# The first norm by token chunks, and the splits of the last merge written two groups later

## The chip, the cores and the metric

One core of a Trainium2 chip runs the kernel. Its engines work side by side: TensorE (PE, matmuls; PEld its weight loads), VectorE (DVE), ScalarE (ACT) and GpSimd (POOL); SyncE (SP) issues most loads. The metric is the device time of one execution in microseconds, the median of several runs. 2331.54 us was measured before the change.

## The reference

One inference step through two layers over 1088 tokens (1024 of a prompt, 64 of eight samples with eight tokens each) and 1024 channels. A layer is:

```python
shift, scale, gate = split(silu(c) @ w_ada + b_ada, 3)
h = rmsnorm(x, norm_g) * (1 + scale) + shift          # rmsnorm: x * rsqrt(mean(x*x) + eps) * g
qa, ka, va, ga, ub, vb, gb, qc, fc, ic, gc, ma, mb, mc = split_cols(h @ w_in)
ya, yb, yc = window_attention(...), spatial_gating(...), hgrn2(...)
merged = sigmoid(ma) * ((ya * silu(ga)) @ w_br_a) + sigmoid(mb) * ((yb * silu(gb)) @ w_br_b) \
       + sigmoid(mc) * ((yc * silu(gc)) @ w_br_c)
x = x + gate * (merged @ w_out)
```

c is one vector for the prompt and one for each sample, so shift, scale and gate have 9 columns: one for all prompt tokens, eight for the samples' tokens. All is float32.

## The kernel before

Activations lie with channels on the 128 partitions and tokens along the free dimension. The 1024 channels are 8 tiles (k = 0 to 7); the 1088 tokens are three chunks (`CH`): chunk 0 and 1 have 384 tokens, chunk 2 has 256 prompt tokens and the 64 sample tokens. A float32 product is made of three fast matmuls (`mm3`, L379 to L381): weights and activations are each split into a high and a low part. For weights a `piece` is cast on ACT (L342) and its low part subtracted on DVE or POOL (L343); for activations `split` does the same (L456 on ACT, L457 on DVE). `H[c]` holds both parts of the normed input of chunk c.

**Order of the work.** POOL and SP follow the program's order throughout (`ORDERED`). PE, DVE and ACT are ordered by a planner with a time model of its own: an engine that is free there gets a ready instruction, and the place in the program ranks those that are ready together. Inside `with tc.manual_schedule(...)` the instructions of PE, DVE and ACT also keep the written order among themselves; those written outside the block may come between them. On the chip each engine then runs its list strictly in order and waits where an operand isn't there. Buffers are rotated: 17 slabs of 1152 columns, 4 raw weight tiles (`wr`), 4 small tiles (`gq`), 4 + 4 banks of PSUM.

**The startup (layer 0).** SP loads the eight tiles of x whole (L1093). ACT squares each (L1096, L1099) and DVE adds the squares up (L1100). `rstd` sums over the partitions with matmuls against a column of ones, one per 128 tokens and nine in all (L473), and finds 1/sqrt in a dozen small DVE steps (L477 to L238). `spread_rows` brings one chunk's factors back over all partitions: a product with the identity on DVE (L489) and a matmul with ones (L491); ACT copies that to `rbs[c]` (L1137). The adaLN factors of channel tile k come from two weight tiles (`ada_load`, two loads of 512 KB), 32 matmuls (L290), an ACT copy (L272), two transposes (L277) and five small DVE operations (L280 to L286). The first unit's weights (`w_first`, four `wr` loads of 256 KB) are loaded ahead of the adaLN weights; POOL makes their low parts.

The loop over k then makes, for each chunk, `modulate` (DVE: x times scale times rbs, L500; for the 64 sample columns three POOL operations, L503 to L506) and `split_h` (ACT adds the shift into the high part, L513; DVE the low part, L514), asks for the adaLN factors of k + 2, and runs 18 matmuls for two output tiles and three chunks. The six sums stay in PSUM over all k. Afterwards the second unit follows with matmuls of another form (L433 to L435).

**The merge.** Three branches, in the order 2, 0, 1; for each 8 output tiles j and 3 chunks, 24 groups of 12 matmuls. After each group `ev_m` asks for a gate two groups ahead (POOL issues the load, L1518), multiplies the gate with the sum in PSUM (DVE, L1549) and adds it to `merged` (POOL, L1550; DVE in the last j). In the third branch the finished tile is split at once (L456, L457), as the output projection's input. Four banks of PSUM hold the sums.

Of the kernel before, what the change touches and what calls it, by code (L numbers as in the profile page):

```python
# [14 lines left out]
AF = mybir.ActivationFunctionType  # L15
# [5 lines left out]
SEQ = 1024  # L21
NB = 8
TS = 8
NTOK = SEQ + NB * TS
# [3 lines left out]
CH = [(0, 384), (384, 384), (768, 320)]  # L28
# [120 lines left out]
def build(tc, i, o, L):  # L149
    nc = tc.nc  # L150
# [8 lines left out]
    V, S, G, T = nc.vector, nc.scalar, nc.gpsimd, nc.tensor  # L159
# [7 lines left out]
    def slab(n="s", dt=F32):  # L167
        return sp.tile([128, 1152], dt, tag="slab", name=uid(n))

    def small(n, w, dt=F32, bufs=2):  # L170
        return sm.tile([128, w], dt, tag=n, name=uid(n), bufs=bufs)
# [7 lines left out]
    def v3(ap, b):  # L179
        return ap.rearrange("p (a b) -> p a b", b=b)  # L180

    def bc_in(ap, n):
        s = list(ap.shape)
        return ap.unsqueeze(len(s)).to_broadcast(s + [n])
# [169 lines left out]
    def prep(parts, eng=V, keep=None):  # L354
        return [piece(p, eng, keep) for p in parts]
# [3 lines left out]
    units = []  # L359
# [24 lines left out]
    nxt = [0]  # L384
# [70 lines left out]
    def split(dst_h, dst_l, src):  # L455
        S.copy(dst_h, src)  # L456
        V.tensor_sub(dst_l, src, dst_h.bitcast(F32))  # L457
# [8 lines left out]
    def rstd(ssq, n):  # L466

        nf, r = n // 128, n % 128
        nt = nf + (r > 0)
        ps = bank("ss")  # L470
        for t in range(nt):
            w = min(128, n - t * 128)
            T.matmul(ps[0:w, t:t + 1], ssq[:, t * 128:t * 128 + w], ones[:, 0:1], start=True, stop=True)  # L473
        vv = small("nv", 9)
        if r:
            V.memset(vv[:, nf:nt], 1.0)
        V.tensor_scalar(vv[:, 0:nf], ps[:, 0:nf], 1.0 / D, EPS, ALU.mult, ALU.add)  # L477
        if r:
            V.tensor_scalar(vv[0:r, nf:nt], ps[0:r, nf:nt], 1.0 / D, EPS, ALU.mult, ALU.add)
        rs = small("nr", 9)  # L480
        rsqrt(vv[:, 0:nt], rs[:, 0:nt], nt)
        return rs

    def spread_rows(rs, n):

        nf, r = n // 128, n % 128
        nt = nf + (r > 0)
        dg = small("gq", 384, bufs=4)
        V.tensor_mul(v3(dg[:, 0:nt * 128], 128), bc_mid(ident, nt), bc_in(rs, 128))  # L489
        pb = bank("rb")  # L490
        T.matmul(pb[:, 0:nf * 128], ones, dg[:, 0:nf * 128], start=True, stop=True)  # L491
        if r:
            T.matmul(pb[:, nf * 128:n], ones[0:64, :], dg[0:64, nf * 128:n], start=True, stop=True)
        return pb

    def modulate(l, k, u, x, rb, t0, n):

        npr = max(0, min(n, SEQ - t0))
        adaT = ada_t[l]
        V.scalar_tensor_tensor(u[:, 0:npr], x[:, 0:npr], adaT[:, 8 + k, 0:1], rb[:, 0:npr], ALU.mult, ALU.mult)  # L500
        if npr < n:
            e = V if l else G
            e.tensor_mul(u[:, npr:n], x[:, npr:n], rb[:, npr:n])  # L503
            us = v3(u[:, npr:n], TS)
            e.tensor_mul(us, us, bc_in(adaT[:, 8 + k, 1:9], TS))
            e.tensor_add(us, us, bc_in(adaT[:, k, 1:9], TS))  # L506

    def split_h(l, k, Hc, u, t0, n):

        npr = max(0, min(n, SEQ - t0))  # L510
        sh = ada_t[l][:, k, 0:1]
        hi, lo = Hc[:, 0, k, :], Hc[:, 1, k, :]
        S.activation(hi[:, 0:npr], u[:, 0:npr], AF.Identity, bias=sh)  # L513
        V.scalar_tensor_tensor(lo[:, 0:npr], u[:, 0:npr], sh, hi[:, 0:npr].bitcast(F32), ALU.add, ALU.subtract)  # L514
        if npr < n:
            S.copy(hi[:, npr:n], u[:, npr:n])
            (V if l else G).tensor_sub(lo[:, npr:n], u[:, npr:n], hi[:, npr:n].bitcast(F32))
# [569 lines left out]


    ada_t = [cp.tile([128, 24, 9], F32, tag=f"adaT{l}", name=f"adaT{l}") for l in range(L)]
    X, ssq = [], slab("ssq")  # L1090
    for k in range(8):
        x = slab("x")
        nc.sync.dma_start(x[:, 0:NTOK], i["xT"][k])  # L1093
        X.append(x)
        if k == 0:
            S.activation(ssq[:, 0:NTOK], x[:, 0:NTOK], AF.Square)  # L1096
        else:
            sq = slab("sq")
            S.activation(sq[:, 0:NTOK], x[:, 0:NTOK], AF.Square)  # L1099
            V.tensor_add(ssq[:, 0:NTOK], ssq[:, 0:NTOK], sq[:, 0:NTOK])  # L1100
    ident = cst("ident", [128, 128])
    ada_consts(0)
    H = new_H()
    rbs = []

    def ada_load(k):
        ws = []
        for a in range(2):
            ws.append(v3(slab("wada")[:, 0:1024], 128))
            nc.sync.dma_start(ws[-1], i["w_ada"][0, 8 * a + k])  # L1110
        return ws

    def ada_both(ps, ws):
        for a in range(2):
            for e in range(2):
                ada_products(ps, a, e, ws[a][:, 4 * e:4 * e + 4])
# [5 lines left out]
            pass  # L1122

    with tc.manual_schedule(engines={ET.PE, ET.DVE, ET.Activation}):
        w_first = prep(units[0], G)
        nxt[0] = 1
        ada_w = [ada_load(0), ada_load(1)]
        rs = rstd(ssq, NTOK)
        ada_ps = bank("ada")
        ada_both(ada_ps, ada_w.pop(0))  # L1130
        for c, (t0, n) in enumerate(CH):
            pb = spread_rows(rs[:, 3 * c:3 * c + 3], n)
            rbs.append(small("gq", 384, bufs=4))
            if c == 0:
                for _ in ada_rows(0, [0, 8], ada_ps):
                    pass
            S.copy(rbs[c][:, 0:n], pb[:, 0:n])  # L1137
    ada_first(1, ada_w.pop(0))
    x_dram = i["xT"]

    for l in range(L):
# [11 lines left out]
        if l == 0:  # L1153

            pss = [[mbank() if m * 3 + c < 4 else bank("first") for c in range(3)] for m in range(2)]
            for k in range(8):
                for c, (t0, n) in enumerate(CH):
                    x = X[k][:, t0:t0 + n]
                    modulate(0, k, x, x, rbs[c], t0, n)
                    split_h(0, k, H[c], x, t0, n)  # L1160
                if k + 2 < 8:
                    ada_first(k + 2, ada_load(k + 2))
                for m in range(2):
                    for c, (t0, n) in enumerate(CH):
                        ps = pss[m][c]
                        rh, rl = rhs_h(c, k)
                        mm3(ps[:, 0:n], col(w_first, 8, m, k), (rh, rl), k == 0, k == 7)
                if k == 3:
                    prefetch()
            for m in range(2):  # L1170
                ev = ev_ga(yd[3][m])
                for c, (t0, n) in enumerate(CH):
                    ev(c, t0, n, pss[m][c][:, 0:n])
            del X, ssq, rbs, x, sq
            late_consts()
            lower_bounds()
            ada_consts(1)
# [14 lines left out]
        k, v = slab("ts"), slab("ts")  # L1192
# [314 lines left out]
        rhs_y = lambda k, c: [cols(t, c) for t in y0[k]]  # L1507


        merged, sgs = [], []  # L1510
        grp = [(b, j, c) for b in BR_ORDER for j in range(8) for c in range(3)]

        def load_gate():
# [7 lines left out]
        for b in range(3):  # L1521
            if b == 0:
                Hy = new_H()
                rhs_n = lambda k, c, Hy=Hy: (Hy[c][:, 0, k, :], Hy[c][:, 1, k, :])
                ly = gated_y(BR_ORDER[1], rhs_n)
                side.append(ly)
            elif b == 1:
                del y0
                y2 = []
                rhs_n = lambda k, c: [cols(t, c) for t in y2[k]]  # L1530
                ly = gated_y(BR_ORDER[2], y2)
                side.append(ly)
            else:
                del Hy
                Hm = new_H()
            for j in range(8):
                if j % 2 == 0:
                    w = unit()
                    M.first = True
                if b == 0:  # L1540
                    merged.append(slab("mg"))

                def ev_m(c, t0, n, ps):
                    load_gate()
                    sg, mg = sgs.pop(0), merged[j][:, t0:t0 + n]
                    if b == 0:
                        V.tensor_mul(mg, sg, ps)  # L1547
                        return
                    V.tensor_mul(sg, sg, ps)  # L1549
                    (V if b == 2 and j == 7 else G).tensor_add(mg, mg, sg)  # L1550
                    if b == 2:
                        split(Hm[c][:, 0, j, :], Hm[c][:, 1, j, :], mg)
                f_mtile(w, j % 2, 4, lambda c, k: rhs_y(k, c), ev_m)
            if b < 2:
                drain(ly)
                rhs_y = rhs_n
        del rhs_y, rhs_n, merged, ly, y2
        drain(*side)
        last = l + 1 == L
        if not last:  # L1560
# [88 lines left out]
```

## Time and profile before

| | us |
|---|---|
| median of 3 runs | 2331.54 (2329.98 to 2332.61) |
| profiled execution | 2331.8 |
| its span, first to last instruction | 2330.0 |
| PE busy | 2257.2 |
| DVE busy | 1273.0 |
| ACT busy | 799.4 |
| POOL busy | 611.5 |

The profile is one execution. The span leaves out 1.8 us around it. Busy time of PE is counted from issue to a modelled end and overlaps, so a count of matmuls in a stretch says more than its busy time. In a timeline row the first number is the start, the second the length, and the bracket says how long the engine had been idle and which instruction ended that.

### The profile page before, as it was taken

The numbers are of one execution on the slowest core, as the hardware profiler recorded it, in microseconds if no ns is written. First come the engines' busy times: TensorE is split into PE (matmuls) and PEld (weight loads), VectorE is DVE, ScalarE is ACT, GpSimd is POOL, SyncE is SP. The second block draws the span as 40 slices with busy tenths as digits, with TensorE's granted clock in tenths as the row PEclk, the third lists the DMA queues.
The fourth block names the chain that finished last, engine by engine and source line by source line (L and its number), as shares of the span: only waits on it lengthen the run. The fifth ranks groups of instructions, "written<-read, shape, count | busy, mean of one in ns | idle before, by whom it ended". The sixth has DMA issues, their size and how long they took to land.

```text
span 2330.0 us, 43307 instructions
## 1 busy us (share of the span) xinstructions
PE 2257.2 (97%) x17170; PEld 2142.1 (92%) x17170; DVE 1273.0 (55%) x2893; ACT 799.4 (34%) x2032; POOL 611.5 (26%) x691
## 2 busy tenths in 40 slices
PE   6999999999999999998999999999999999999998
PEld 5999899989999899997999988999899999999898
DVE  6557748575363435464573586576654633346431
ACT  4436622333133334122243465223331433332110
POOL 3101014242232322275110010132322332315621
PEclk9999999999999999999999999999999999999999
DMA  7222110203134445664422121112121323366541
GB/s 285 78 81 68 62 50 25 85 29 117 47 117 153 159 161 200 223 204 132 131 91 78 62 76 65 37 48 67 59 86 60 107 89 110 107 229 204 156 132 46
DMA packets 128442, 251.26 MB, mean 108 GB/s; under 512 B 19760, under 2 KB 59952, under 8 KB 128208
## 3 DMA queue, kind: packets, MB, share of 16 engines
q1 hardware_dynamic: 87824, 156.46, 21.0%
q0 software_dynamic: 19680, 65.29, 8.4%
q10 hardware_dynamic: 20736, 26.75, 3.2%
q8 instruction: 135, 2.21, 0.4%
q14 instruction: 67, 0.55, 0.1%
HBM read 185.13 MB, written 65.27 MB: 107 GB/s over the span
## 4 chain that ended last, share of the span: by engine, by line
PE 65%; DVE 11%; issue 9%; POOL 8%; DMA 3%; ACT 2%; SPq 1%; POOLq 0%; DVEq 0%; ACTq 0%
PE mm L379 13%; PE mm L380 13%; PE mm L381 12%; PE mm L433 4%; POOL mg L1550 4%; PE mm L435 4%; PE mm L434 4%; PE c L379 2%; PE c L381 2%; PE c L380 2%; POOL gq L1518 1%; PE av L914 1%; DVE pc L343 1%; DMA wr<-in_w_in 1%; PE sc L877 1%
## 5 line engine op out<-in xcount | busy, mean ns | idle before, releaser
L379 PE MATMUL mm<-H,pc 128*128 128x384 f32 (+1 forms) x1872 | 626.5, 335 | 5.8 <-DVE gq L1549 4.7
L380 PE MATMUL mm<-H,pc 128*128 128x384 f32 (+1 forms) x1872 | 614.6, 328 | 0.0
L381 PE MATMUL mm<-H,pc 128*128 128x384 f32 (+1 forms) x1872 | 614.5, 328 | 0.0
L343 DVE TENSOR_TENSOR pc<-wr,pc 128x512 fp32r<-128x512 f32 x308 | 223.5, 739 | 295.8 <-ACT pc L342 294.7
L379 PEld LDWEIGHTS mm<-H,pc 128*128 128x128 f32 x1872 | 352.3, 188 | 27.2 <-issue 16.5
L380 PEld LDWEIGHTS mm<-H,pc 128*128 128x128 f32 x1872 | 352.6, 188 | 3.8 <-issue 3.2
L381 PEld LDWEIGHTS mm<-H,pc 128*128 128x128 f32 x1872 | 352.1, 188 | 1.1 <-DVE H L457 0.6
L433 PE MATMUL mm<-pc,H 128*128 128x256 f32 x896 | 259.0, 289 | 0.2 <-DVE gq L1150 0.2
L435 PE MATMUL mm<-pc,H 128*128 128x256 f32 x896 | 254.4, 284 | 0.0
L434 PE MATMUL mm<-pc,H 128*128 128x256 f32 x896 | 253.6, 283 | 0.0
L342 ACT CAST pc<-wr 128x512 fp32r<-128x512 f32 x312 | 189.7, 620 | 162.2 <-PE mm L381 80.0
L435 PEld LDWEIGHTS mm<-pc,H 128*128 128x128 f32 x896 | 171.6, 192 | 3.2 <-issue 3.2
L433 PEld LDWEIGHTS mm<-pc,H 128*128 128x128 f32 x896 | 171.6, 192 | 2.3 <-DVE gq L1150 0.5
L434 PEld LDWEIGHTS mm<-pc,H 128*128 128x128 f32 x896 | 171.7, 192 | 0.0
L379 PE MATMUL mm<-y,pc 128*128 128x384 f32 (+1 forms) x384 | 128.3, 334 | 15.7 <-DVE gq L1549 15.7
L381 PE MATMUL mm<-y,pc 128*128 128x384 f32 (+1 forms) x384 | 125.5, 327 | 0.0
L380 PE MATMUL mm<-y,pc 128*128 128x384 f32 (+1 forms) x384 | 125.3, 326 | 0.0
L1550 POOL TENSOR_TENSOR mg<-mg,gq 128x384 f32<-128x384 f32 (+1 forms) x90 | 103.4, 1149 | 77.1 <-DVE gq L1549 74.9
L457 DVE TENSOR_TENSOR tw<-wr,tw 128x512 fp32r<-128x512 f32 x80 | 65.6, 850 | 94.4 <-ACT tw L456 94.3
L631 POOL TENSOR_TENSOR hk<-hk,ht 128x512 f32<-128x512 f32 (+1 forms) x48 | 70.1, 1462 | 136.2 <-issue 39.8
L1151 POOL DMA_DIRECT2D y<-gq x48 | 26.4, 551 | 289.1 <-DVE gq L1150 116.3
L1518 POOL DMA_DIRECT2D gq<-g x144 | 79.2, 551 | 85.0 <-DVE mg L1547 50.4
(413 smaller groups left out, 4491.3 us busy)
## 6 DMA issues: line engine op xcount, KB each, us to landing
wr<-in_w_in SPq DMA_DIRECT2D x192, 256.0 KB, 3.3
yr<-y SPq DMA_DIRECT2D x40, 544.0 KB, 4.6
g<-gq ACTq DMA_DIRECT2D x96, 192.0 KB, 1.9
gq<-g POOLq DMA_DIRECT2D x96, 192.0 KB, 2.9
wada<-in_w_ada SPq DMA_DIRECT2D x64, 256.0 KB, 3.6
wr<-in_w_in SPq DMA_DIRECT2D x112, 128.0 KB, 2.5
wr<-in_w_br SPq DMA_DIRECT2D x48, 256.0 KB, 5.3
wada<-in_w_ada SPq DMA_DIRECT2D x16, 512.0 KB, 7.4
```

The source lines that it names most:

```text
L342: S.copy(pc[:, 0, :], flat)
L343: eng.tensor_sub(pc[:, 1, :], flat, pc[:, 0, :].bitcast(F32))
L379: T.matmul(ps, w[0], r[0], start=start, stop=False, skip_group_check=True)
L380: T.matmul(ps, w[1], r[0], start=False, stop=False, skip_group_check=True)
L381: T.matmul(ps, w[0], r[1], start=False, stop=stop, skip_group_check=True)
L433: T.matmul(p3(ps), a, wh[k], start=k == 0, stop=False)
L434: T.matmul(p3(ps), a, wl[k], start=False, stop=False)
L435: T.matmul(p3(ps), b, wh[k], start=False, stop=k == 7)
L457: V.tensor_sub(dst_l, src, dst_h.bitcast(F32))
L631: G.tensor_mul(kv[:, :, 0, :], kv[:, :, 0, :], bc_in(tv[:, :, 1], m))
L1518: nc.gpsimd.dma_start(sgs[-1], gd[b][j][:, t0:t0 + n])
L1550: (V if b == 2 and j == 7 else G).tensor_add(mg, mg, sg)
```

## The change

1. x is loaded chunk by chunk (`x_load`), 24 loads instead of 8. Chunk 0 comes first, then the adaLN weights of k = 0, chunk 1, the adaLN weights of k = 1, the first unit's weights, chunk 2.
2. Squares, sums, `rstd` and the spreading run once per chunk (`x_stats`), in written order: chunk 0, then the adaLN factors of k = 0 and the casts of the first weights, then chunk 1, then chunk 2.
3. Chunks 1 and 2 of all eight x tiles are multiplied with `rbs` by POOL, in place, 16 operations. In the loop ACT applies scale and shift in one Identity, in place, and the plain `split` follows. The sample columns keep two POOL operations per k. Chunk 0 is made as before.
4. In the third branch of the merge the split of a group is written after the evacuation of the group two later; the last two follow after the loop.

```diff
--- before.py
+++ after.py
@@ -1087,17 +1087,26 @@
 
 
     ada_t = [cp.tile([128, 24, 9], F32, tag=f"adaT{l}", name=f"adaT{l}") for l in range(L)]
-    X, ssq = [], slab("ssq")
-    for k in range(8):
-        x = slab("x")
-        nc.sync.dma_start(x[:, 0:NTOK], i["xT"][k])
-        X.append(x)
-        if k == 0:
-            S.activation(ssq[:, 0:NTOK], x[:, 0:NTOK], AF.Square)
-        else:
-            sq = slab("sq")
-            S.activation(sq[:, 0:NTOK], x[:, 0:NTOK], AF.Square)
-            V.tensor_add(ssq[:, 0:NTOK], ssq[:, 0:NTOK], sq[:, 0:NTOK])
+    X = [slab("x") for _ in range(8)]
+
+    def x_load(c):
+        t0, n = CH[c]
+        for k in range(8):
+            nc.sync.dma_start(X[k][:, t0:t0 + n], i["xT"][k][:, t0:t0 + n])
+
+    def x_stats(c):
+
+        t0, n = CH[c]
+        q = slab("ssq")[:, 0:n]
+        for k in range(8):
+            if k % 3 == 0:
+                sq = slab("sq")
+            d = sq[:, k % 3 * 384:k % 3 * 384 + n] if k else q
+            S.activation(d, X[k][:, t0:t0 + n], AF.Square)
+            if k:
+                V.tensor_add(q, q, d)
+        return rstd(q, n)
+    x_load(0)
     ident = cst("ident", [128, 128])
     ada_consts(0)
     H = new_H()
@@ -1122,19 +1131,27 @@
             pass
 
     with tc.manual_schedule(engines={ET.PE, ET.DVE, ET.Activation}):
-        w_first = prep(units[0], G)
-        nxt[0] = 1
-        ada_w = [ada_load(0), ada_load(1)]
-        rs = rstd(ssq, NTOK)
+        ada_w = [ada_load(0)]
+        x_load(1)
+        ada_w.append(ada_load(1))
         ada_ps = bank("ada")
-        ada_both(ada_ps, ada_w.pop(0))
         for c, (t0, n) in enumerate(CH):
-            pb = spread_rows(rs[:, 3 * c:3 * c + 3], n)
+            rs = x_stats(c)
+            if c == 0:
+                ada_both(ada_ps, ada_w.pop(0))
+            pb = spread_rows(rs[:, 0:3], n)
             rbs.append(small("gq", 384, bufs=4))
+            S.copy(rbs[c][:, 0:n], pb[:, 0:n])
             if c == 0:
                 for _ in ada_rows(0, [0, 8], ada_ps):
                     pass
-            S.copy(rbs[c][:, 0:n], pb[:, 0:n])
+                w_first = prep(units[0], G)
+                nxt[0] = 1
+                x_load(2)
+            else:
+                for k in range(8):
+                    x = X[k][:, t0:t0 + n]
+                    G.tensor_mul(x, x, rbs[c][:, 0:n])
     ada_first(1, ada_w.pop(0))
     x_dram = i["xT"]
 
@@ -1156,8 +1173,17 @@
             for k in range(8):
                 for c, (t0, n) in enumerate(CH):
                     x = X[k][:, t0:t0 + n]
-                    modulate(0, k, x, x, rbs[c], t0, n)
-                    split_h(0, k, H[c], x, t0, n)
+                    if c == 0:
+                        modulate(0, k, x, x, rbs[c], t0, n)
+                        split_h(0, k, H[c], x, t0, n)
+                        continue
+                    npr, at = min(n, SEQ - t0), ada_t[0]
+                    S.activation(x[:, 0:npr], x[:, 0:npr], AF.Identity, bias=at[:, k, 0:1], scale=at[:, 8 + k, 0:1])
+                    if npr < n:
+                        us = v3(x[:, npr:n], TS)
+                        G.tensor_mul(us, us, bc_in(at[:, 8 + k, 1:9], TS))
+                        G.tensor_add(us, us, bc_in(at[:, k, 1:9], TS))
+                    split(H[c][:, 0, k, :], H[c][:, 1, k, :], x)
                 if k + 2 < 8:
                     ada_first(k + 2, ada_load(k + 2))
                 for m in range(2):
@@ -1171,7 +1197,7 @@
                 ev = ev_ga(yd[3][m])
                 for c, (t0, n) in enumerate(CH):
                     ev(c, t0, n, pss[m][c][:, 0:n])
-            del X, ssq, rbs, x, sq
+            del X, rbs, x
             late_consts()
             lower_bounds()
             ada_consts(1)
@@ -1507,7 +1533,7 @@
         rhs_y = lambda k, c: [cols(t, c) for t in y0[k]]
 
 
-        merged, sgs = [], []
+        merged, sgs, late_split = [], [], []
         grp = [(b, j, c) for b in BR_ORDER for j in range(8) for c in range(3)]
 
         def load_gate():
@@ -1549,12 +1575,16 @@
                     V.tensor_mul(sg, sg, ps)
                     (V if b == 2 and j == 7 else G).tensor_add(mg, mg, sg)
                     if b == 2:
-                        split(Hm[c][:, 0, j, :], Hm[c][:, 1, j, :], mg)
+                        late_split.append((Hm[c][:, 0, j, :], Hm[c][:, 1, j, :], mg))
+                        if len(late_split) > 2:
+                            split(*late_split.pop(0))
                 f_mtile(w, j % 2, 4, lambda c, k: rhs_y(k, c), ev_m)
             if b < 2:
                 drain(ly)
                 rhs_y = rhs_n
-        del rhs_y, rhs_n, merged, ly, y2
+        for x in late_split:
+            split(*x)
+        del rhs_y, rhs_n, merged, ly, y2, late_split, x
         drain(*side)
         last = l + 1 == L
         if not last:
```

## Rows read from the trace of the kernel before

**Rows 1.** The page's part 1: busy us, share, instructions.
```profile
PE 2257.2 (97%) x17170; PEld 2142.1 (92%) x17170; DVE 1273.0 (55%) x2893; ACT 799.4 (34%) x2032; POOL 611.5 (26%) x691
```

**Rows 2.** Timeline of the startup: start us, length us, engine, line, operation.
```profile
5.13 1.11 ACT L1096 ACTIVATE ssq<-x 128x1088 f32<-128x1088 f32 x1 [2.37 <-DMA x<-in_xT]
14.71 1.11 ACT L1099 ACTIVATE sq<-x 128x1088 f32<-128x1088 f32 x1 [0.33 <-DMA x<-in_xT]
15.73 2.59 ACT L342 CAST pc<-wr 128x512 fp32r<-128x512 f32 x4
16.43 5.69 POOL L343 TENSOR_TENSOR pc<-wr,pc 128x512 fp32r<-128x512 f32 x4 [15.37 <-ACT pc L342]
17.36 3.87 PE L473 MATMUL ss<-ones,ssq 128*128 128x1 f32 x18 [17.36 <-DVE ssq L1100]
24.23 0.56 DVE L489 TENSOR_TENSOR gq<-c_ident,nr 128x384 f32<-128x384 f32 x1
24.84 1.65 PE L491 MATMUL rb<-gq,ones 128*128 128x384 f32 x2 [1.75 <-DVE gq L489]
29.81 0.79 PE L379 MATMUL mm<-H,pc 128*128 128x384 f32 x1
```

**Rows 3.** Windows: length; busy us (count) of PE, PEld, DVE, ACT, POOL.
```profile
36.20:69.30 33.10, 32.15 (x318) 28.39 (x315) 31.79 (x93) 20.39 (x46) 12.01 (x27) 1.00 0.47 146
```

**Rows 4.** Groups by line, 36 to 69.3: count, busy us, mean ns.
```profile
L500 DVE SCALAR_TENSOR_TENSOR x<-x,adaT,gq 128x384 f32<-128x384 f32 x14 | 9.1, 661 | 0.0
L514 DVE SCALAR_TENSOR_TENSOR H<-x,adaT,H 128x384 fp32r<-128x384 f32 x14 | 8.6, 619 | 0.9 <-ACT H L513 0.9
L505 POOL TENSOR_TENSOR x<-x,adaT 128x64 f32<-128x64 f32 x7 | 3.7, 533 | 14.1 <-DVE adaT L284 14.1
L506 POOL TENSOR_TENSOR x<-x,adaT 128x64 f32<-128x64 f32 x7 | 2.6, 368 | 0.5
```

**Rows 5.** Timeline of the last merge, layer 0, two groups.
```profile
1083.74 0.55 DVE L1549 TENSOR_TENSOR gq<-gq,mm 128x384 f32<-128x384 f32 x1
1084.38 1.00 POOL L1550 TENSOR_TENSOR mg<-mg,gq 128x384 f32<-128x384 f32 x1 [1.07 <-DVE gq L1549]
1085.42 0.52 ACT L456 CAST H<-mg 128x384 fp32r<-128x384 f32 x1 [2.12 <-POOL mg L1550]
1085.97 0.56 DVE L457 TENSOR_TENSOR H<-mg,H 128x384 fp32r<-128x384 f32 x1 [1.68 <-ACT H L456]
1086.44 0.55 DVE L1549 TENSOR_TENSOR gq<-gq,mm 128x384 f32<-128x384 f32 x1
1086.91 0.68 DVE L1576 TENSOR_TENSOR wol<-wr,woh 128x512 fp32r<-128x512 f32 x1
1087.08 1.39 POOL L1550 TENSOR_TENSOR mg<-mg,gq 128x384 f32<-128x384 f32 x1 [1.19 <-DVE gq L1549]
```

**Rows 6.** Windows, a stretch of the output projection at 384 columns.
```profile
1106.00:1130.00 24.00, 24.00 (x141) 24.00 (x140) 11.48 (x21) 6.99 (x14) 3.73 (x7) 1.00 0.47 149
```

**Rows 7.** Windows, the last merge of each layer.
```profile
1050.00:1098.00 48.00, 40.06 (x218) 35.13 (x216) 21.29 (x42) 13.05 (x26) 28.32 (x36) 1.00 0.47 143
2180.00:2226.00 46.00, 38.23 (x210) 33.79 (x208) 20.52 (x40) 12.53 (x25) 27.89 (x34) 1.00 0.46 142
```

**Rows 8.** Groups by line, 1106 to 1200: squares of the next norm.
```profile
L1609 ACT ACTIVATE u<-x 128x384 f32<-128x384 f32 x14 | 7.4, 527 | 38.8 <-DVE x L1597 38.8
L1609 ACT ACTIVATE u<-x 128x320 f32<-128x320 f32 x7 | 3.3, 474 | 9.0 <-DVE x L1602 9.0
```

**Rows 9.** Groups by line, POOL, whole span.
```profile
L1277 POOL TENSOR_TENSOR ub<-ub,gq 128x384 f32<-128x384 f32 x16 | 16.3, 1016 | 78.7 <-DVE gq L1275 78.7
```

**Rows 10.** Timeline around 673 us: POOL and DVE side by side.
```profile
672.71 1.33 POOL L1320 TENSOR_TENSOR st<-H 128x384 f32<-128x384 f32 x1
673.08 1.37 DVE L1328 TENSOR_TENSOR st<-st 128x384 f32<-128x384 f32 x1
674.37 0.55 DVE L1319 TENSOR_TENSOR st<-H 128x384 f32<-128x384 f32 x1
```

## The prediction

> **What bounds the kernel now.** I read the page first: PE is busy 97% of the span [rows 1], so only what leaves PE waiting can change the time. Then I followed the two stretches that the diff touches in the timeline and in the windows.
>
> The startup: eight tiles of x (557 KB each) land from 5.13 to 14.71 us, one every 1.37 us, which is 407 GB/s; then come the squares, one statistics chain for all nine token tiles (PE 3.87, small DVE steps until 24.23, the diagonal product 0.56, the spreading matmul 1.65), and the first main matmul at 29.81 [rows 2]. From 36.2 to 69.3 PE runs 318 matmuls, and DVE is busy 31.79 of 33.1 us [rows 3]: PE and DVE are both near their limit there. At 69.3 the second unit begins. The reader is to see that DVE spends a modulate (0.66) and a low part (0.62) for each chunk and k [rows 4].
>
> The last merge: one group goes multiply 0.55 (DVE), add 1.00 (POOL), high part 0.52 (ACT), low part 0.56 (DVE), and only then the next multiply, 1083.74 to 1086.44, 2.70 us a group [rows 5]; DVE's low part had waited 1.68 us. PE needs 12 matmuls a group; at the 24.00/141 = 0.170 us each of the output projection [rows 6] that is 2.04 us at 384 columns and, scaled, 1.70 at 320. In 1050 to 1098 PE ran 218 matmuls and in 2180 to 2226 210 [rows 7]: 428 of them, a third at 320 columns, need 428 x 0.161 = 68.9 of the 94 us. So some 25 us, 12 to 13 in each layer, are lost to this wait.
>
> **The late splits.** They remove no instruction; they are written two groups later. Whether that brings back the 25 us hangs on who orders DVE. There the order is the planner's, which gives an engine what is ready by its own clock, and the program's order decides only between two that are ready together. Rows 5 show it: the low part of an output weight (L1576), written after the whole merge, runs at 1086.91 between a multiply and that group's own split. DVE was free, so the planner took it. The same holds for a split: its inputs are ready at the same planned moment, wherever it is written, and at that moment DVE has nothing else, since the next multiply waits for PE. In the planner's clock the split was ready before the next multiply in group after group. On the chip it is later, because POOL's 1.00 us add holds it. I therefore take 0 for this part; the other end is the whole 25. If the wait goes, POOL is next: add 1.0 plus a gate load's issue, still under PE's period.
>
> **The startup, part by part.**
> - Loads: 8 x loads become 24, the bytes stay. Ahead of the first weights now lie chunk 0 and chunk 1 of x (1.57 MB each) and two pairs of adaLN weights (1.05 MB each). With the weights' own 1.05 MB that is 6.29 MB; at 407 GB/s from 3.75 us (5.13 less one tile) the last piece is there at 19.2, its cast (0.65, a quarter of 2.59) done at 19.9. Before, casts ended at 18.3 [rows 2]. SP issues 16 more loads; the transfers are the slower part and cover them.
> - Chunk 0: its x is there at 7.6 instead of 14.7, and its chain measures 3 token tiles, not 9 (1.29 for 3.87 on PE). Its H leads by about 10 us, and the weights become the later of the two: POOL's four low parts took 5.69 [rows 2], so the first matmul comes near 20 instead of 29.8.
> - Chunk 1: in ACT's written order its squares stand behind the casts, which wait for the weights. From 19.9: squares 8 x 0.53 [rows 8], last add 0.56 (as the subtract of that size in rows 5), PE 1.29, the small DVE steps 3.0 (21.23 to 24.23), product 0.6, spreading 1.65, copy 0.5: scale ready at 31.7.
> - Chunk 2: its squares stand behind that copy. 8 x 0.47 [rows 8], last add 0.47 (scaled to 320 columns), then the same 1.29 + 3.0 + 0.6 + 1.65 + 0.45: ready at 43.0 with nothing in the way.
> - POOL gets 16 scalings. One at 384 columns takes 1.02 [rows 9], so at 320 about 0.85. In POOL's written order the 16 small operations on the sample columns come behind all of them, mean 0.53 and 0.37 beside a busy DVE [rows 4].
> - DVE gives up the 16 modulates of chunks 1 and 2, their low parts become plain subtracts, and it keeps chunk 0. ACT gets an Identity and a copy where it had one pass. Neither is the end of the chain below, but DVE stands in it.
>
> **The price of sharing.** POOL and DVE slow each other when DVE reads two tiles in SBUF: an add of POOL with nothing beside it takes 1.00 and beside L1576 it takes 1.39 [rows 5]; where 384-column operations of both follow each other, POOL's takes 1.33 and DVE's 1.37 instead of the 0.55 of the next one, and DVE starts one every 1.29 us [rows 10]. So 1.02 + 0.55 = 1.57 us of work, each alone, takes 1.29 together, a factor of 0.82.
> The Trainium skill (GPSIMD Engine Reference, section 1, Specifications) says that GpSimd shares its SBUF interfaces with VectorE and that they contend when DVE has two SBUF inputs. This trace agrees as far as these rows go: L1576 and L1328 read two tiles in SBUF, and both cost POOL time. By that rule every squared sum, low part and modulate of the startup meets POOL's scalings, and eight of these at 384 columns take 8 x 1.33 = 10.6 us; by rows 9 alone they take 8.2.
>
> Two sums follow. Along the chain: chunk 2's scale at 43.0, or at 48.3 if its seven adds run beside POOL's chunk 1 (7 x 1.37 = 9.6 for 4.3); POOL's eight scalings 6.8 to 10.6; its small operations 16 x 0.37 = 5.9 to 8 x 0.90 = 7.2; copy, low part and six matmuls, scaled to 320 columns, 0.45 + 0.47 + 0.85 = 1.8. The stretch would end between 57.5 and 67.9.
> By the shared work: POOL has 5.7 (weights) + 8.2 + 6.8 + 5.9 = 26.6. DVE with two SBUF inputs has 14 adds 7.2, chunk 0 8 x 1.28 = 10.2, low parts 8 x (0.56 + 0.47) = 8.2, the next unit's four pieces 4 x 0.68 = 2.7, two products 1.1: 29.4. Together 56.0 x 0.82 = 45.9 from POOL's first weight at about 18.5: 64.4, and 1.3 for the last copy and matmuls: 65.7, if neither engine ever pauses. Both do: POOL has nothing from its last weight (18.5 + 5.7 = 24.2) to chunk 1's scale at 31.7, and again while chunk 2's chain sits on PE and in small steps (1.29 + 3.0 + 0.6 + 1.65 = 6.5), 14 us in all; DVE fills part of that with chunk 0, and at other times waits, in order, for POOL's products. I take 8 us of pauses: 73.7, against 69.3 now, **+4.4 us**. It is the larger of the two sums because both must hold. After this stretch nothing changes, and the loss stays in the end time. Against the profiled execution (2331.8, span 2330.0 and 1.8 around it) that is 2336.2; the median shown is 0.3 lower, so I forecast **2335.9**.
>
> **Rivals.**
> 1. *The late splits work.* For it: the wait stands in group after group of both layers, and at equal readiness the new order would decide. Against: L1576 in rows 5, as said. It would give 2335.9 less 25 = 2311; with a startup that costs nothing, 2307. Not slower. Chance 0.20.
> 2. *The startup gains.* DVE's idle gaps take the shared work, chunk 0 and 1 feed PE from 20 us on, and chunk 2 ends by the chain alone, at 62 to 67: 2 to 7 us faster, 2327. For it: PE's main matmuls start 9 us earlier. Against: DVE is full already. Chance 0.13.
> 3. *The startup loses much more.* The planner counts POOL too cheap (its splits came later on the chip than planned), so it queues DVE and PE on chunk 2 ahead of chunk 0's last k; in-order engines then stand behind POOL. With the pauses at 15 instead of 8 the end is 80.7: +11.4, 2342.9. It decides if work of chunk 0 or 1 stands behind chunk 2's. Chance 0.25.
>
> **How the numbers follow.** The forecast has 0.42, with a range of its own from 2332 to 2341 (pauses of 4 to 13 us). About 0.2%, 4.7 us, is what a measurement of this kernel can tell from no change. Faster by more than that: rival 1 and a third of rival 2, 0.25. Slower: rival 3 and 0.2 of the forecast's 0.42, 0.45. The rest is 0.30. The range 2308 to 2345 takes in most of rival 1 and of rival 3 and leaves out about 0.15.
>
> **What would show it.** In the changed profile: the first main matmul near 20; the squares of chunk 1 behind the casts; POOL's scalings at 1.2 us or more; DVE adds of chunk 2 over 1 us; the second unit's first matmul at 71 to 77. In the merge: the same 2.7 us a group and some 218 matmuls in 48 us. I am wrong if the second unit begins before 67, or if a multiply follows a multiply without a split's wait between them.

## The result, and the profile after

The changed kernel is slower: 2354.11 us (median of 4 runs, 2351.80 to 2357.12) against 2332.07 for the kernel before in the same series, a ratio of 1.0096 with a 95% interval of 1.0083 to 1.0108. The profiled execution took 2353.64 us, its span 2351.9 against 2330.0: 21.9 us more. Every engine does nearly the work it did before; the page's part 1 answers to [rows 1]:

```profile
PE 2259.2 (96%) x17170; PEld 2142.1 (91%) x17170; DVE 1276.7 (54%) x2915; ACT 805.3 (34%) x2056; POOL 623.4 (27%) x691
```

So the 21.9 us are waiting, and the question is where PE waits. The merge is as it was. The two windows that answer to [rows 7], moved to where the merges lie now, hold 217 and 208 matmuls, for 218 and 210:

```profile
1072.60:1120.60 48.00, 39.88 (x217) 34.96 (x216) 21.47 (x43) 13.08 (x26) 28.14 (x36) 1.00 0.45 142
2202.00:2248.00 46.00, 38.11 (x208) 33.32 (x206) 20.52 (x40) 12.60 (x26) 27.87 (x34) 1.00 0.46 143
```

and one group of the timeline still shows VectorE's low part (L457) waiting 1.68 us for its input, ahead of the next multiply (L1575 here), as in [rows 5]:

```profile
1106.18 0.55 DVE L1575 TENSOR_TENSOR gq<-gq,mm 128x384 f32<-128x384 f32 x1
...
1106.82 1.01 POOL L1576 TENSOR_TENSOR mg<-mg,gq 128x384 f32<-128x384 f32 x1 [1.07 <-DVE gq L1575]
...
1107.86 0.51 ACT L456 CAST H<-mg 128x384 fp32r<-128x384 f32 x1 [2.12 <-POOL mg L1576]
...
1108.40 0.56 DVE L457 TENSOR_TENSOR H<-mg,H 128x384 fp32r<-128x384 f32 x1 [1.68 <-ACT H L456]
...
1108.88 0.55 DVE L1575 TENSOR_TENSOR gq<-gq,mm 128x384 f32<-128x384 f32 x1
```

All of it is in the startup. The second unit's first matmul (L433) stands at 92.9 us instead of 69.3 [rows 3]: 23.6 us later. The view of that line up to 110 us in the kernel before and in the changed one (count; shortest, median and longest ns; first and last start; forms):

```profile
L433 PE MATMUL mm<-pc,H x104: 280/283/387, 69.3 to 109.5; 128*128 128x256 f32 x104
...
L433 PE MATMUL mm<-pc,H x48: 281/283/283, 92.9 to 109.8; 128*128 128x256 f32 x48
```

This is the startup's timeline (start, length, engine, line, operation; in brackets the idle time before it and what ended it), the answer to [rows 2]:

```profile
16.56 0.48 ACT L1144 COPY gq<-rb 128x384 f32<-128x384 f32 x1 [7.58 <-PE rb L491]
...
22.20 1.97 ACT L342 CAST pc<-wr 128x512 fp32r<-128x512 f32 x3 [0.19 <-DMA wr<-in_w_in]
...
24.07 0.52 ACT L1105 ACTIVATE ssq<-x 128x384 f32<-128x384 f32 x1
...
27.39 0.60 ACT L513 ACTIVATE H<-x,adaT 128x384 fp32r<-128x384 f32 x1
...
28.04 0.69 PE L379 MATMUL mm<-H,pc 128*128 128x384 f32 x1 [9.98 <-ACT H L513]
...
37.68 0.48 ACT L1144 COPY gq<-rb 128x384 f32<-128x384 f32 x1 [9.69 <-PE rb L491]
...
38.24 9.41 POOL L1154 TENSOR_TENSOR x<-x,gq 128x384 f32<-128x384 f32 x8 [10.89 <-ACT gq L1144]
...
38.92 7.87 DVE L1107 TENSOR_TENSOR ssq<-ssq,sq 128x320 f32<-128x320 f32 x7 [3.04 <-ACT sq L1105]
...
53.17 0.43 ACT L1144 COPY gq<-rb 128x320 f32<-128x320 f32 x1 [10.99 <-PE rb L493]
...
53.67 6.92 POOL L1154 TENSOR_TENSOR x<-x,gq 128x320 f32<-128x320 f32 x8 [6.03 <-ACT gq L1144]
...
60.56 0.29 POOL L1184 TENSOR_TENSOR x<-x,adaT 128x64 f32<-128x64 f32 x1
...
60.93 0.29 POOL L1185 TENSOR_TENSOR x<-x,adaT 128x64 f32<-128x64 f32 x1
...
61.26 0.46 ACT L456 CAST H<-x 128x320 fp32r<-128x320 f32 x1 [4.10 <-POOL x L1185]
...
61.77 0.47 PE L379 MATMUL mm<-H,pc 128*128 128x320 f32 x1 [4.09 <-ACT H L456]
```

The reader is to see three things. The scales of the three chunks are copied at 16.56, 37.68 and 53.17, one chain after the other; before, the last copy was done at 32.9. Between 53.67 and 60.59 POOL scales all of chunk 2. Only then come the two sample operations of k = 0 (L1184, L1185), and ACT (4.10 us idle) and PE (4.09) wait for exactly these: the matmul at 61.77 is k = 0, chunk 2. PE then needs nearly as long as ever. In the windows, the stretch before that matmul holds 86 matmuls, the one behind it 305, with PE busy throughout, as the 318 in 33.1 us of [rows 3]. The first line is the last copy in the kernel before:

```profile
32.43 0.43 ACT L1137 COPY gq<-rb 128x320 f32<-128x320 f32 x1 [1.63 <-PE rb L493]
...
36.20:61.70 25.50, 10.73 (x86) 6.88 (x86) 14.63 (x29) 6.58 (x17) 17.28 (x20) 1.00 0.51 161
61.70:92.90 31.20, 31.14 (x305) 28.48 (x306) 25.69 (x86) 25.29 (x55) 8.11 (x14) 0.95 0.35 112
...
63.00:65.00 2.00, 2.00 (x18) 1.63 (x20) 1.91 (x5) 1.72 (x4) 1.03 (x2) 0.50 0.95 365
...
67.00:70.00 3.00, 3.00 (x43) 2.81 (x45) 2.63 (x9) 2.64 (x6) 1.22 (x2) 1.00 0.43 123
```

The last two rows show a smaller cost of the wait: after PE had stood idle from 57.7 to 61.7, its granted clock (the first number behind POOL's) was at the lower level, 1.2 GHz or 0.50, from 63 to 65, and back at 2.4 GHz, 1.00, from 67 on. With a mean of 0.95 over 31.2 us that is an estimated 1.6 us.

### The profile page after: what moved, and what is told of

The parts are those of the page before. It is cut to its first block, busy times and chain, and to the rows that moved or that the text cites. A ratio compares the mean times of both kernels' runs of the same rounds, so it can differ in the third digit from the quotient of the medians.

```text
span 2351.9 us, 43366 instructions
## 1 busy us (share of the span) xinstructions
PE 2259.2 (96%) x17170; PEld 2142.1 (91%) x17170; DVE 1276.7 (54%) x2915; ACT 805.3 (34%) x2056; POOL 623.4 (27%) x691
## 3 DMA queue, kind: packets, MB, share of 16 engines
q1 hardware_dynamic: 90128, 156.46, 20.6%
## 4 chain that ended last, share of the span: by engine, by line
PE 66%; DVE 10%; POOL 9%; issue 9%; DMA 4%; ACT 2%; SPq 0%; POOLq 0%; DVEq 0%; ACTq 0%
PE mm L379 13%; PE mm L380 13%; PE mm L381 12%; PE mm L433 4%; PE mm L435 4%; POOL mg L1576 4%; PE mm L434 4%; PE c L381 2%; PE c L379 2%; PE c L380 2%; POOL gq L1544 1%; PE av L914 1%; PE sc L877 1%; DVE pc L343 1%; DMA wr<-in_w_in 1%
## 5 line engine op out<-in xcount | busy, mean ns | idle before, releaser
L379 PEld LDWEIGHTS mm<-H,pc 128*128 128x128 f32 x1872 | 351.9, 188 | 46.8 <-issue 16.6
L433 PE MATMUL mm<-pc,H 128*128 128x256 f32 x896 | 259.6, 290 | 0.0
L433 PEld LDWEIGHTS mm<-pc,H 128*128 128x128 f32 x896 | 172.3, 192 | 1.8
L457 DVE TENSOR_TENSOR tw<-wr,tw 128x512 fp32r<-128x512 f32 x80 | 65.6, 850 | 94.2 <-ACT tw L456 94.1
```

Source lines behind the costliest of these rows:

```text
L379: T.matmul(ps, w[0], r[0], start=start, stop=False, skip_group_check=True)
L433: T.matmul(p3(ps), a, wh[k], start=k == 0, stop=False)
```

## The experiments

Two theories came first. A: the order of work is the loss; PE, DVE and ACT have k = 1 to 7 behind the last chunk's statistics. B: POOL's 16 scalings and their sharing with DVE are the loss. Neither held as it stood; after seven runs a third, C, took their place. Each kernel's time is compared with the kernel before on the same chip; "second unit" is the start of its first matmul in the profile.

**The late splits alone** (e1), on the kernel before:

```diff
+ late_split.append((Hm[c][:, 0, j, :], Hm[c][:, 1, j, :], mg))
+ if len(late_split) > 2:
+     split(*late_split.pop(0))
```

> The kernel before with the late splits alone. Theory A (all of the loss lies in the startup; writing a split later changes nothing where the planner orders the engines by readiness): within 3 us of before, 2329 to 2335, and the same wait of some 1.7 us ahead of the low parts in the last merge. Rival (the late splits do bring back some of the 25 us, and the startup lost that much more): 2307 to 2322.

Measured: ratio 1.000 (0.9989 to 1.0011), and the wait stays:

```profile
1086.60 1.00 POOL L1550 TENSOR_TENSOR mg<-mg,gq 128x384 f32<-128x384 f32 x1 [1.07 <-DVE gq L1549]
...
1087.63 0.51 ACT L456 CAST H<-mg 128x384 fp32r<-128x384 f32 x1 [2.12 <-POOL mg L1550]
```

In the two programs the planner's list for VectorE differs by one exchange of neighbours in 2893 instructions, and those of the other engines not at all. Where a split is written has next to no effect on the order here, and none on the time.

**The same splits, held in place** (e6):

```diff
- V.tensor_mul(sg, sg, ps)
+ mul = V.tensor_mul(sg, sg, ps)
...
+ with tc.issue_after(mul.ins):      # DVE's part stands behind this multiply
+     split(*late_split.pop(0))
```

> The kernel before with the late splits and an order that holds: DVE's low part of a group is tied behind the multiply of the group two later. If the wait in the last merge is the low part standing ahead of the next multiply, PE gets its 12 to 13 us back in each layer: 2305 to 2312. Rival: the adds and gate loads on GpSimd (1.57 us of busy time a group) take over as the limit, or slow beside DVE: 2315 to 2325. If the low part isn't what PE waits for: 2330 to 2334.

Measured: 2309.46 against 2332.56, ratio 0.9907 (0.9888 to 0.9925). In the timeline, the multiply and the low part of an older group now follow each other without a wait:

```profile
1085.61 0.54 DVE L1549 TENSOR_TENSOR gq<-gq,mm 128x384 f32<-128x384 f32 x1
...
1086.07 0.55 DVE L457 TENSOR_TENSOR H<-mg,H 128x384 fp32r<-128x384 f32 x1
```

and PE runs 287 matmuls in the window of [rows 7] that held 218 (249 of the merge; the other 38 are the output projection's, which now begins within the window):

```profile
1050.00:1098.00 48.00, 47.60 (x287) 47.28 (x286) 36.83 (x60) 16.85 (x34) 32.31 (x40) 1.00 0.53 165
```

This version beats both kernels: 23 us faster than before, some 45 than the changed one.

**VectorE scales** (e5), the changed kernel without POOL's scalings:

```diff
- G.tensor_mul(x, x, rbs[c][:, 0:n])        # chunks 1 and 2
...
+ modulate(0, k, x, x, rbs[c], t0, n)       # all chunks
+ split_h(0, k, H[c], x, t0, n)
```

> The changed kernel, but VectorE modulates chunks 1 and 2 as it did before, so the 16 scalings on GpSimd are gone; the statistics stay one chunk after the other in written order. Theory A (PE, DVE and ACT have the work of k = 1 to 7 behind the statistics of the third chunk, so that chain sets the loss, whoever scales): still slow, 2347 to 2358; the adds of chunk 2 fall from 1.1 to about 0.55 us and the chain ends some 4 us earlier, but DVE gets 10 us of work back in the loop. Theory B (GpSimd's scalings and their sharing with DVE are the loss): most of it comes back, 2332 to 2342.

Measured: 1.0079 (1.0064 to 1.0094), second unit at 88.0. In ACT's timeline the last scale is copied at 50.57 + 0.43 = 51.0:

```profile
50.57 0.43 ACT L1144 COPY gq<-rb 128x320 f32<-128x320 f32 x1 [8.15 <-PE rb L493]
```

The loop takes 37.0 us from there, as it took 36.4 before (32.9 to 69.3). With no scaling on POOL at all, four fifths of the loss stay: theory B can't be the whole. The time, 2351.93, lies in theory A's range.

**Chunks as the outer loop** (e7):

```diff
- for k in range(8):
-     for c, (t0, n) in enumerate(CH):
+ for c, (t0, n) in enumerate(CH):
+     for k in range(8):
...
+         if c == 0 and k in (1, 4):
+             lead(1 if k == 1 else 2)        # statistics of that chunk
```

> The changed kernel with the chunk as the outer loop: the adaLN factors and chunk 0's matmuls of all k come first, the statistics of chunk 1 are written after k = 1 of chunk 0 and those of chunk 2 after k = 4, outside the block of written order; GpSimd scales chunks 1 and 2 as in the changed kernel. Theory A (order): chunk 0's matmuls and the adaLN products fill PE from 28 us on, and the second unit begins at 66 to 78 instead of 92.9: 2327 to 2339. Theory B (GpSimd and DVE sharing): POOL still has its 16 scalings of 1.2 us and DVE waits for them, the second unit begins after 87: 2348 or more.

Measured: 1.0103 (1.0088 to 1.0118), second unit at 91.4. Theory A missed. Theory B's figures came out (after 87, 2348 or more), but not by its mechanism: POOL's two sets of scalings took 8.60 and 6.65 us and POOL stood idle for 16 us between them. Chunk 0's matmuls did come forward (the first at 24.24), and from POOL's last scaling (77.9) to the second unit it was 13.5 us, not 32. But chunk 2's statistics, written later, ended later: its scale was copied at 71.2. Loads of the adaLN weights also waited for slabs, but up to 60 us they did so for 20.4 us here and for 23.3 in the changed kernel (SP's waits of L1119 for L290 and L1107), so this doesn't tell the two apart.

In 28.0 to 57.4 PE was busy 17.87 us, at a mean granted clock of 0.77 between its two levels of 1.2 and 2.4 GHz. The edit changed too much at once to part the theories; smaller ones followed.

**Two groups of statistics** (e10): chunks 1 and 2 together, so one chain fewer.

```diff
- t0, n = CH[c]
+ t0, n = CH[c] if c == 0 else (384, 704)
...
- rs = x_stats(c)
+ if c < 2:
+     rs = x_stats(c)
```

> The changed kernel with two groups instead of three: chunk 0 leads, the squares, sums and statistics of chunks 1 and 2 are done together (704 columns), so one chain of small steps fewer stands in series. Theory A (the loop over k begins when the last chunk's scale is copied to rbs, and takes 36 to 39 us from there: 32.9 to 69.3 before, 53.6 to 92.9 in the changed kernel, 51.0 to 88.0 where DVE scales): the last copy comes at 41 to 45, the second unit begins at 79 to 83, time 2340 to 2346. Theory B (GpSimd's 16 scalings of 1.2 us and their sharing set the loss): 16 of them from 40 us on end near 58 as they do in the changed kernel, time 2350 or more.

Measured: 1.0080 (1.0065 to 1.0095), second unit at 88.0. The last copy came as theory A had it, at 42.8, but the second unit moved by 4.9 us where 10 to 14 were expected. The time, 2353.21, and the end of POOL's scalings, 56.0, came out nearer to theory B. POOL's timeline shows why:

```profile
40.80 15.20 POOL L1154 TENSOR_TENSOR x<-x,gq 128x384 f32<-128x384 f32 x16 [14.14 <-ACT gq L1144]
...
42.44 0.40 ACT L1144 COPY gq<-rb 128x320 f32<-128x320 f32 x1
...
55.97 0.61 POOL L1184 TENSOR_TENSOR x<-x,adaT 128x64 f32<-128x64 f32 x1
...
56.98 0.46 ACT L456 CAST H<-x 128x320 fp32r<-128x320 f32 x1 [4.63 <-POOL x L1185]
```

Scaling ends at 56.0, and from there to the second unit it is 32.0 us; in the changed kernel it is 60.6 to 92.9, 32.3.

**All squares first** (e4): only chunk 0 in the block of written order.

```diff
+ def lead(c):                # a chunk's statistics, its spreading, POOL's scalings
...
+     lead(0)                 # in the block
...
+ lead(1)                     # behind the block
+ lead(2)
```

> The changed kernel with only chunk 0 in the block of written order; chunks 1 and 2 follow it in the program, and the planner then puts all 24 squares on ScalarE ahead of the casts of the first weights. Chunk 2 of x lands at 27.05 as in the changed kernel. Theory A: the last chunk's scale is copied at 35 to 40 instead of 53.6, the second unit begins 36 to 39 us later at 72 to 79, time 2333 to 2340. Theory B (GpSimd): POOL's scalings start after chunk 1's scale and need 17 to 19 us, the second unit begins after 85, time 2346 or more.

Measured: 1.0102 (1.0085 to 1.0119), second unit at 94.5. Theory A missed; theory B's figures came out (2357.53, and 18.6 us from the start to the end of POOL's scalings), though POOL stood idle for 4 us between its two sets. With all 24 squares ahead in ACT's list, chunk 0's own scale was copied at 32.34 instead of 16.56, the others at 42.97 and 54.67: the chains stayed in series. And here the sharing did lengthen a chain: chunk 2's small steps ran beside POOL's scalings of chunk 1 and took 7.9 us (43.92 to 51.81) where in e5, with POOL idle, they took 2.4 (45.60 to 47.98). The last section shows them. The end of POOL's scaling (62.1) to the second unit is 32.4 us again.

**POOL's scaling alone** (e9), on the kernel before, statistics in one chain:

```diff
  S.copy(rbs[c][:, 0:n], pb[:, 0:n])
+ if c:
+     for k in range(8):
+         x = X[k][:, t0:t0 + n]
+         G.tensor_mul(x, x, rbs[c][:, 0:n])
```

> The kernel before with the third part of the change alone: x is loaded whole and the statistics are one chain as before, but GpSimd scales chunks 1 and 2 (16 operations, chunk 1 first) and ScalarE applies scale and shift. Theory A: the scale of chunk 2 is there at 33 as before; POOL's 8 scalings of chunk 1 hold chunk 2's first tile until about 42, then PE is the limit again, second unit at 72 to 76: 2331 to 2339. Theory B (the scalings and the sharing are the loss of 22 us): 2346 to 2356.

Measured: 1.0043 (1.0028 to 1.0058), second unit at 79.9: between the two theories. Here the last scale is there at 33.4, and the loop still begins at 48:

```profile
31.32 15.23 POOL L1141 TENSOR_TENSOR x<-x,gq 128x384 f32<-128x384 f32 x16 [8.76 <-ACT gq L1137]
...
46.51 0.61 POOL L1171 TENSOR_TENSOR x<-x,adaT 128x64 f32<-128x64 f32 x1
...
47.20 0.30 POOL L1172 TENSOR_TENSOR x<-x,adaT 128x64 f32<-128x64 f32 x1
...
47.53 0.46 ACT L456 CAST H<-x 128x320 fp32r<-128x320 f32 x1 [4.64 <-POOL x L1172]
...
48.04 0.63 PE L379 MATMUL mm<-H,pc 128*128 128x320 f32 x1 [1.47 <-ACT H L456]
```

That gave theory C: PE's list has all three chunks of k = 0 ahead of k = 1, chunk 2 of k = 0 needs the sample columns, POOL has these behind its last scaling, and the whole loop, 32 to 33 us, runs after that. Four more runs put it to the test.

**Scalings tile by tile** (e12), e9 with POOL's operations in the order of k:

```diff
- for k in range(8): ...                      # the 16 scalings ahead of the loop
...
+ G.tensor_mul(x, x, rbs[c][:, 0:n])          # in the loop, ahead of the Identity
```

> Like e9 (the kernel before, statistics in one chain, GpSimd scales chunks 1 and 2), but the scalings stand tile by tile in the loop: chunk 1, chunk 2, then the two sample operations of that k, about 2.8 us a tile against 4.3 us that PE needs. Theory C: k = 0 is complete at 36 as in the kernel before, the second unit begins at 70 to 73 instead of 79.9, time 2331 to 2336. Rival B (16 scalings beside DVE cost this by the sharing alone, in whatever order): second unit after 77, time 2341 or more.

Measured: 1.0014 (1.0004 to 1.0024), second unit at 72.7: theory C, 7.2 us back by the edit of order alone; the time, 2338.06, is 2 us over the range given. Not all of the 7.2 is the wait itself: e9's loop ran at a mean granted clock of 0.90, e12's at 1.00, an estimated 31.9 x 0.10 = 3.2 us. The 3.4 us that remain against the kernel before fit the sharing: the loop takes 36.5 us with 320 matmuls where it took 33.1 with 318 [rows 3], and in it VectorE's low part of 384 columns takes 836 ns for 619 in [rows 4]:

```profile
48.00:79.90 31.90, 31.70 (x301) 28.72 (x302) 24.80 (x79) 24.16 (x51) 8.40 (x14) 0.90 0.26 66
...
36.20:72.70 36.50, 32.49 (x320) 28.44 (x315) 33.34 (x90) 24.88 (x53) 21.36 (x27) 1.00 0.45 135
...
L514 DVE SCALAR_TENSOR_TENSOR H<-x,adaT,H 128x384 fp32r<-128x384 f32 x7 | 5.9, 836 | 1.8 <-ACT H L513 1.8
```

**Both legs** (e13): e10 with the scalings tile by tile, an edit as in e12.

> Like e10 (chunk 0 leads, chunks 1 and 2 as one group of statistics, last scale copied at 42.8), with the scalings tile by tile in the loop. Theory C: k = 0 is complete at about 46, the second unit begins at 78 to 81 instead of 88.0, time 2339 to 2344: the rest against the kernel before is then the later end of the statistics, 42.8 for 32.9. Rival B: second unit after 85, time 2348 or more.

Measured: 1.0057 (1.0042 to 1.0072), second unit at 82.5, 5.5 us earlier than in e10 and 1.5 later than theory C's range. The time, 2346.40, lies between the two ranges too, nearer to B's, so C holds for the gain but not for the whole of its size. From 46.5 on PE ran 308 matmuls in 36.0 us, about e12's pace, as POOL's scalings stand in this loop as well.

**Only chunk 2 by tiles** (e11), the changed kernel:

```diff
- else:
+ elif c == 1:
      for k in range(8): ...                  # chunk 1 scaled ahead
...
+ if c == 2:
+     G.tensor_mul(x, x, rbs[c][:, 0:n])      # in the loop
```

> The changed kernel, but GpSimd's scaling of chunk 2 is written inside the loop, tile by tile, so that k = 0's two operations on the sample columns no longer stand behind all eight scalings. Theory C (PE's list has all three chunks of k = 0 ahead of k = 1, chunk 2 of k = 0 needs the sample columns, and these stand behind POOL's last scaling; the whole loop of 32 to 33 us then runs after it: last scaling's end to second unit 60.6 to 92.9 in the changed kernel, 46.6 to 79.9 in e9, 56.0 to 88.0 in e10, 62.1 to 94.5 in e4): the loop begins 5 us earlier, the second unit at 87 to 90, time 2347 to 2351. Rival D (the loop waits for the adaLN factors of k = 1, written behind the last statistics and done at 58, not for POOL): second unit at 91 to 93, time 2352 to 2355.

Measured: second unit at 89.3, as C had it; the ratio, 1.0092 (1.0075 to 1.0109), can't be told from the changed kernel's, and the time, 2355.18, missed C's range and lies at the end of D's. Chunk 2's first tile leaves POOL at 55.27, but its matmul starts at 57.68, behind the adaLN products of k = 1 and 2 in PE's list, so the loop begins 4.1 us earlier (61.77 before the edit) though the tile is there 6.0 us earlier (61.22 before the edit): a part of rival D holds.

```profile
53.05 3.19 PE L290 MATMUL ada<-wada,cT 128*32 128x128 f32 x50
...
54.98 0.29 POOL L1187 TENSOR_TENSOR x<-x,adaT 128x64 f32<-128x64 f32 x1
...
57.68 0.42 PE L379 MATMUL mm<-H,pc 128*128 128x320 f32 x1
```

**The casts behind chunk 1's squares** (e15), the changed kernel:

```diff
- if c == 0: ...
-     w_first = prep(units[0], G)
+ rs = x_stats(c)
+ if c == 1:
+     w_first = prep(units[0], G)
```

> The changed kernel with ScalarE's four casts of the first weights written behind chunk 1's squares instead of ahead of them (the loads keep their order). Theory C (the statistics of the three chunks stand in series behind the casts, and their end sets when the loop begins): chunk 1's squares run at 17 to 21, its scale is copied at 28 to 31 instead of 37.7, the last at 43 to 47 instead of 53.2, the second unit begins at 82 to 87 instead of 92.9, time 2343 to 2349. Rival (the squares' place behind the casts costs nothing, since chunk 1's small steps on VectorE or its x are late anyway): last copy after 51, time 2352 or more.

Measured: 1.0078 (1.0060 to 1.0095), second unit at 89.6, last copy at 49.1. The squares ran at 17.2 to 20.6, but the scale of chunk 1 was copied at 33.2 where 28 to 31 were expected; the last copy, the second unit and the time (2354.48) all missed theory C's ranges, and the time lies in the rival's. Some 2 us were lost on VectorE, beside POOL's low parts: L477's result is there at 26.59, and the next step of the chain, L232, ends at 28.83, behind an L514 of 1.17 us and after 1.23 of its own:

```profile
22.89 5.91 POOL L343 TENSOR_TENSOR pc<-wr,pc 128x512 fp32r<-128x512 f32 x4 [21.84 <-DMA wr<-in_w_in]
...
26.43 0.16 DVE L477 TENSOR_SCALAR nv<-ss 128x3 f32<-128x3 f32 x1 [1.53 <-PE ss L473]
...
26.50 1.17 DVE L514 SCALAR_TENSOR_TENSOR H<-x,adaT,H 128x384 fp32r<-128x384 f32 x1
...
27.60 1.23 DVE L232 TENSOR_SCALAR rs_i<-nv 128x3 int32<-128x3 int32 x1
...
28.86 0.17 DVE L233 TENSOR_SCALAR nr<-rs_i 128x3 int32<-128x3 int32 x1
```

**Tiles and held splits** (e14): e12 with e6's edit.

> e12 with the late splits held in their place as in e6: the two stretches lie apart, so the gain of e6 (23 us) should add in full to whatever e12 shows: e12's time less 22 to 24 us, 2308 to 2313 if e12 equals the kernel before, and then no better than e6 (2309.5).

Measured: 2316.04, ratio 0.9924 (0.9909 to 0.9939), 22.0 us under e12. The gain of the merge adds in full. e6 stays the lowest, though the two intervals overlap.

The times follow the second unit in every startup, within 2.1 us. The last column is the ratio's excess over 1 times 2332. In e1 and e6, whose startup is the one before, the second unit stands at 70.0 and 70.2, so differences under 1 us say nothing:

| kernel | last scale copied | POOL's last scaling ends | second unit | later than 69.3 by | time |
|---|---|---|---|---|---|
| changed | 53.6 | 60.6 | 92.9 | 23.6 | +22.4 |
| e4 | 55.1 | 62.1 | 94.5 | 25.2 | +23.8 |
| e10 | 42.8 | 56.0 | 88.0 | 18.7 | +18.7 |
| e9 | 33.4 | 46.6 | 79.9 | 10.6 | +10.0 |
| e15 | 49.1 | 55.8 | 89.6 | 20.3 | +18.2 |
| e5 | 51.0 | none | 88.0 | 18.7 | +18.4 |
| e7 | 71.2 | 77.9 | 91.4 | 22.1 | +24.0 |
| e11 | 53.6 | in the loop | 89.3 | 20.0 | +21.5 |
| e12 | 33.2 | in the loop | 72.7 | 3.4 | +3.3 |
| e13 | 42.8 | in the loop | 82.5 | 13.2 | +13.3 |

From the end of the scaling to the second unit it is 32.0 to 33.8 us in the five kernels that go by k with the scalings ahead.

## Why the prediction was wrong

**The step that failed** is the end of the chain: "copy, low part and six matmuls, scaled to 320 columns, 0.45 + 0.47 + 0.85 = 1.8", with the stretch ending "between 57.5 and 67.9", and the shared work (73.7) as the larger sum. It took for granted that PE has done everything else by the time that chunk 2's last tile arrives. It hadn't: PE's list goes by k, and its second tile begins behind the first tile's chunk 2. Behind POOL's last scaling stand not six matmuls but 31.2 us of PE work (305 matmuls). With 53.6 + 7.0 + 32.3 the chain would have given 92.9. The price of sharing and DVE's pauses, on which the forecast was built, were not what set the end; DVE is busy only 14.63 of 25.5 us ahead of the loop. That the sign came out as forecast (slower, by 4.4 us) is no support for that sum.

**Rival 3** named the mechanism, "in-order engines then stand behind POOL", and its condition ("if work of chunk 0 or 1 stands behind chunk 2's"), but priced it by longer pauses, +11.4. The measured price is 22. What was missing was a count of what stands behind: k = 1 to 7 of every chunk, and the adaLN products of k = 3 to 7.

**Other terms.** Casts done: predicted 19.9, measured 24.2; the 6.29 MB ahead came slower than the 407 GB/s of [rows 2] (337 on the average of 6 to 24.2 us). First matmul: predicted near 20, measured 28.04; its high part (L513) stood behind chunk 1's eight squares in ACT's list, where the text let the weights decide. Chunk 1's scale: 31.7, measured 38.2, of which 4.3 are the casts. Chunk 2's scale: 43.0 to 48.3, measured 53.6; the step itself, 15.4 us, lies in the 11.3 to 16.6 given, and in e5, without POOL's scalings beside it, it takes 12.0: so the sharing lengthened the chain by 3.4 us. POOL's eight scalings of chunk 2: 6.8 to 10.6, measured 6.92, the lower end; DVE ran only six operations beside them, 3.55 us in all. Chunk 2's adds beside POOL: over 1 us, measured 7.87/7 = 1.12.

**How the 23.6 us divide.** The last scale comes 20.7 us later (32.9 to 53.6). From there to the second unit it was 36.4 us and is 39.3: POOL's seven us of scaling stand in front, and the loop behind them is shorter. Where POOL's order plays no part, the second unit follows the last scale almost one for one: 18.1 us later copy and 18.7 later unit in e5 against the kernel before, 9.6 and 9.8 in e13 against e12. One chain fewer takes 10.8 us from the first part (e10), the casts behind the squares 4.5 (e15). POOL's scaling by itself, on the kernel before, costs 10.6 us, of which 7.2 go with its order and 3.4 with the sharing (e9 and e12); in the changed kernel, chunk 2's order alone is worth 3.6 (e11).

**Right:** the late splits at nothing, for the reason given (e1); and the other end, 25 us, if the order did change: e6 gives 23.

What stays open: why the adaLN weights and x landed slower in pieces (the DMA engines were busy for 0.99 of 6 to 24.2 us, as for 1.03 of 6 to 18 before), and whether an order of the startup exists that beats the one before; the runs here don't show one.

## What to carry to other kernels

When a change delays one input of an in-order list, price everything that stands behind it in that list, not the operation that needs it; find the first waiting instruction and count what follows. Moving work to an idle engine moves that engine's order too: in e9 two small operations behind sixteen large ones cost more than the sharing of the two engines did. And where a planner orders an engine by readiness, writing a step later may change nothing, as in e1; tying it behind an instruction changed the time, in e6.

## What the runs showed of the hardware

A small VectorE operation beside a running POOL operation can take as long as POOL's. In e4, chunk 2's steps on 128x3 ran beside POOL's scalings of chunk 1, which took 7.68/8 = 0.96 us each. From 44.58 to 51.23 seven of them took 0.92 or 0.93 us each, where in e5, with POOL idle, they take 0.16 or 0.17. L477, which reads PSUM, kept its 0.16:

```profile
43.53 7.68 POOL L1150 TENSOR_TENSOR x<-x,gq 128x384 f32<-128x384 f32 x8 [4.90 <-ACT gq L1146]
...
43.92 0.16 DVE L477 TENSOR_SCALAR nv<-ss 128x2 f32<-128x2 f32 x1 [1.91 <-PE ss L473]
...
44.58 0.93 DVE L233 TENSOR_SCALAR nr<-rs_i 128x3 int32<-128x3 int32 x1
```

In e15 L232 took 1.23 us and ended at 28.83, with POOL's four subtracts ending at 28.80. L232 and L233 read one tile in SBUF, so two SBUF inputs aren't needed for it. The Trainium skill (SBUF — State Buffer, section "SBUF: two separate sides") calls the port pair that the two share an exclusive lock, held for a whole instruction by whichever starts first, and counts VectorE's two-port modes in. That L232 and L233 ran in such a mode no run here shows. By the rule of the lock, an add of 320 columns (0.48 in e5, where POOL is idle) and a scaling of 384 (0.99 for the first in e12, where VectorE is idle) would take 0.99 + 0.48 = 1.47 us a pair, an estimate; in the changed kernel they took 9.41/8 = 1.18 and 7.87/7 = 1.12. The trace agrees that they delay each other, but part of the two still runs together.
